# A transformer kernel on one core: a convolution's sums in a PSUM bank, and other lo parts and PSUM banks at six places

## The chip, the cores and the metric

The kernel runs on one core of a Trainium2 chip. The metric is the device time of one execution in microseconds (us). Before the change the median of three runs is 2507.14 us (2504.99 to 2510.89).

The engines' names are those of the profile: PE is TensorE (PEld its weight loads), DVE VectorE, ACT ScalarE, POOL GpSimd, SP the engine that issues most DMAs. Each engine executes its instructions in a fixed order and waits where an operand or a buffer is not ready.

## The reference

Two layers over 512 tokens of width 1024, in fp32. The first block holds an even and an odd layer; each is an attention mixer, a layer norm, an FFN with a squared ReLU and a gated embedding (PLE). The second block is an RWKV7 mixer beside a convolution branch, and another FFN. The convolution branch, which the change touches, is a gated unit and a causal depthwise convolution over 31 tokens:

```
u   = a * sigmoid(b)                    # [tokens, channels], a and b are projections
y_t = bias + sum_{j=0..30} w[:, j] * u_{t-30+j}
```

The gate of the PLE is `x + sigmoid(h @ W_gate + b) * (e @ W_proj)` with a 1024x1024 W_gate.

## The kernel before

**Arithmetic.** Each fp32 product is three fp32r matmuls (mm3, L290 to L292): hi by hi, and the two mixed products of a hi part and a lo part. So each weight needs a hi part (the value rounded to fp32r) and a lo part (the remainder). A weight arrives in parts of 128x1024 values: SP issues the DMA into wraw (L265), ACT writes the hi part whi (L267), and the lo part wlo comes in one of two ways (load_part):

- eng is None: ACT writes the negated hi part into wlo (L270), and POOL's queue issues a DMA (L271) that adds wraw to it on arrival.
- eng is DVE or POOL: that engine subtracts, wraw less whi (L273).

With fast=True the parts of one weight alternate between DVE and POOL, whatever eng is.

**Order.** The tile framework's scheduler writes out one static order for each engine from the program below, its pools' buffer counts and its own costs. A PSUM tag such as psm is a set of banks of 128x512 fp32 values, taken in rotation; a new use waits until the last reader of the old content is done.

**First block.** even_mixer ends with out_proj of ev_w_out, whose second half of columns (256 to 511) is loaded at L782. ffn_and_ple then runs ffn and the gate. The gate's weight comes in two halves of 512 columns (c = 0, 1 at L645 to L647), each in four parts; the first half has fast=True. In ffn, up(0) uses first_two (L419 to L428), which fills two PSUM banks over two halves of the tokens and between them calls the two postponed norms late[0] and late[1]; their transposes (L347) go to psa banks and are copied out by ACT (L351) and DVE (L352). up(1), up(2) and so on take psm banks, which ACT reads with the ReLU (L440). There are three FFNs in the program: two in the first block, one in the second.

**Second mixer.** second_block gives it eight PSUM banks: three psm, one psd, two pst, one psq, one pso (L1721). Eight rounds, one for each 128 channels, weave the RWKV part (projections shifted by shift_add, L1121 and L1122, and wkv_proj, L1449 to L1506) with conv_chunk. In conv_chunk two projections (psd) make the gated unit u (glu, L1401); ACT writes the first tap with the bias into cacc (L1403), and DVE adds the other 30 taps, one instruction each (L1406), 240 in all:

```
    for j in range(1, 31):
        nc.vector.scalar_tensor_tensor(acc, u[:, j:j + 512], cw[:, fc * 31 + j:fc * 31 + j + 1], acc,
                                       op0=ALU.mult, op1=ALU.add)
```

POOL then adds cacc to a running sum (L1343, L1345) and SP stores it.

Of the kernel before, what the change touches and what calls it, by code (L numbers as in the profile page):

```python
# [13 lines left out]
AF = mybir.ActivationFunctionType  # L14
# [274 lines left out]
def mm3(nc, ps, w, x, first, last):  # L289
    nc.tensor.matmul(ps, w[0], x[0], start=first, stop=False)  # L290
    nc.tensor.matmul(ps, w[0], x[1], start=False, stop=False)  # L291
    nc.tensor.matmul(ps, w[1], x[0], start=False, stop=last)  # L292
# [110 lines left out]
def ffn(g, w_up, w_down, X, alpha, hp, tmp, late, norm, fm=None, fill=None):  # L403
# [7 lines left out]
    nc = g.nc  # L411
# [6 lines left out]

    def first_two(W):  # L419

        pss = [g.ps("psm") for _ in range(2)]
        for half, t in enumerate(HALF_TOKENS):
            for e, ps in enumerate(pss):
                for kc in range(8):
                    w = tuple(a[:, e * 128:e * 128 + 128] for a in W[kc])
                    mm3(nc, ps[:, t], w, (X[0][:, kc, t], X[1][:, kc, t]), kc == 0, kc == 7)
                if half == 0:
                    late[e]()  # L428
        return pss
# [162 lines left out]
def ffn_and_ple(g, l, X, late):  # L592

    nc, tc, d = g.nc, g.tc, g.d
    with ExitStack() as s2:
        g.psum(s2, psa=4, psu=2, psm=2)
        pp = g.pool(s2, "ple", 1, side="right")
        up = g.pool(s2, "pleu", 5, side="right")
        pb = g.bcast_row(pp, f"ple_b{l}")
        U = {}  # L600

        def embed(c):

            Wp = g.load_w(d[f"ple_w_proj{l}"][:, c * 512:c * 512 + 512])
            for tb in range(4):
                ps = g.ps("psa")
                for kc in range(2):
                    mm3(nc, ps, tuple(a[:, tb * 128:tb * 128 + 128] for a in P[kc]), Wp[kc], kc == 0, kc == 1)
                U[c, tb] = up.tile([128, 512], F32, name="pu", tag="pu")
                nc.scalar.activation(U[c, tb], ps, AF.Copy, scale=0.5)  # L610

        with ExitStack() as s3:
            hp = g.pool(s3, "hp", 3)
            tmp = g.pool(s3, "ftmp", 1)
            br = g.pool(s3, "brow", 1)
            norm, fm = norm_fm(g, br, l, "ln2", X, "psm", "psm")
            P = []

            def fill():
                P.extend(g.load_w(d["pT"][l]))  # L620
                embed(0)

            late = ffn(g, d[f"w_up{l}"], d[f"w_down{l}"], X, ALPHA, hp, tmp, late, norm, fm, fill)
        tmp = g.pool(s2, "ptmp", 3, side="right")
        if l == 1:
            hn = g.pool(s2, "mhn", 2, side="right")
            gb = g.bcast_row(pp, "norm_mix", "brow2")

        def after(tb):
            if l == 0:  # L630
                to_fm(g, g.x[tb], X, tb)
            else:
                nc.scalar.dma_start(g.xd[tb * 128:tb * 128 + 128, :], g.x[tb])
                ht = hn.tile([128, D], F32, name="hn", tag="hn")
                rms_norm_tm(g, g.x[tb], ht, gb, g.v1[:, V1["eps6"][0]:V1["eps6"][1]])
                to_fm(g, ht, X, tb)

        if l == 0:
            zero = tmp.tile([128, 512], F32, name="zero", tag="pt")
            nc.gpsimd.memset(zero, 0.0)  # L640
            md = g.md.rearrange("k b x -> (k b x)").rearrange("(p x) -> p x", p=128)
            for j in range(0, 1040, 512):
                n = min(512, 1040 - j)
                nc.sync.dma_start(md[:, j:j + n], zero[:, 0:n])
        for c in range(2):  # L645
            cs = slice(c * 512, c * 512 + 512)
            Wg = g.load_w(d[f"ple_w_gate{l}"][:, cs], fast=c == 0, eng=nc.gpsimd)  # L647
            for tb in range(4):
                if c == 0 and 0 < tb < 3:
                    late[tb - 1]()  # L650
                ps = proj_tm(g, Wg, X, tb)
                t = tmp.tile([128, 512], F32, name="pt", tag="pt")
                nc.vector.tensor_tensor(t, ps, pb[:, cs], op=ALU.add)
                nc.scalar.activation(t, t, AF.Tanh, scale=0.5)
                nc.vector.scalar_tensor_tensor(t, t, 1.0, U[c, tb], op0=ALU.add, op1=ALU.mult)
                xs = g.x[tb][:, cs]
                nc.vector.tensor_tensor(xs, xs, t, op=ALU.add)
                if c == 1 and tb > 0:
                    after(tb - 1)
            if c == 0:  # L660
                embed(1)
        after(3)
# [94 lines left out]
def even_mixer(g, outer, late, X, load_x):  # L757
    d, nc = g.d, g.nc
    with ExitStack() as st:
        g.psum(st, psm=2, pst=2, psv=1, pss=3)  # L760
        g.weight_pools(st, 3, 3)
        OT = g.pool(st, "evo", 1).tile([128, 8, 512], F32, name="oT")
        W0 = load_x()
        with ExitStack() as s2:
            a = g.pool(s2, "ev", 1)
            cq, ckv, rq, rkv, rkvb = latents(g, a, X, W0)
            ap = g.pool(s2, "att", 3)
            cs = a.tile([128, 1152], F32, name="cs")
            csk = ap.tile([128, 512], F32, name="tq", tag="tq", bufs=2)
            nc.sync.dma_start(csk, d["ce"][:, OE["cs_k"][0]:OE["cs_k"][1]])  # L770
            nc.sync.dma_start(cs[:, 1024:1152], d["ce"][:, OE["sum4"][0]:OE["sum4"][1]])
            nc.sync.dma_start(cs[:, 0:1024], d["ce"][:, OE["cs_e"][0]:OE["cs_o"][1]])
            win = window_heads(g, a, ap, X, OT)
            lat = latent_heads(g, a, ap, X, OT, cq, ckv, rq, rkv, rkvb, cs, csk)
            units = []
            for p in range(4):
                units += win[2 * p:2 * p + 2] + lat[2 * p:2 * p + 2]
            pipeline(units)
        W = [g.load_w(d["ev_w_out"][:, 0:256])]
        g.alloc_x(outer)  # L780
        g.weight_pools(late, *FFN_W, side="right")
        W.append(g.load_w(d["ev_w_out"][:, 256:512]))  # L782
        load_tokens(g)
        order = [4, 0, 5, 1, 6, 2, 7, 3]
        for j in order:
            split_sb(g, OT[:, j, :], X[0][:, j, :], X[1][:, j, :], nc.vector)
        return out_proj(g, d["ev_w_out"], W, X, ALPHA, "pss", *norm_fm(g, g.pool(st, "evn", 1), 0, "ln1", X, *LATE_TAGS), order)
# [604 lines left out]
def conv_chunk(g, fc, ka, vv, cw, H, cn):  # L1392

    nc, d = g.nc, g.d
    pb = yield from proj_steps(g, d["w_in"][:, 4096 + fc * 128:4224 + fc * 128], H, "psd", fc == 0, fc < 2)
    t = ka.tile([128, 512], F32, name="glt", tag="glt")
    nc.scalar.activation(t, pb, AF.Tanh, scale=0.5)
    pa = yield from proj_steps(g, d["w_in"][:, 3072 + fc * 128:3200 + fc * 128], H, "psd", fc == 0)
    u = ka.tile([128, 542], F32, name="glu", tag="glu")
    nc.vector.memset(u[:, 0:30], 0.0)  # L1400
    nc.vector.scalar_tensor_tensor(u[:, 30:542], t, 1.0, pa, op0=ALU.add, op1=ALU.mult)  # L1401
    acc = ka.tile([128, 512], F32, name="cacc", tag="cacc", bufs=2)
    nc.scalar.activation(acc, u[:, 0:512], AF.Identity, scale=cw[:, fc * 31:fc * 31 + 1],  # L1403
                         bias=vv("conv_b")[:, fc:fc + 1])
    for j in range(1, 31):
        nc.vector.scalar_tensor_tensor(acc, u[:, j:j + 512], cw[:, fc * 31 + j:fc * 31 + j + 1], acc,  # L1406
                                       op0=ALU.mult, op1=ALU.add)
    cn.add(fc, acc)

# [307 lines left out]
def second_block(g, out):  # L1717
    nc, tc, d = g.nc, g.tc, g.d
    with ExitStack() as st:
        with ExitStack() as s2:  # L1720
            g.psum(s2, psm=3, psd=1, pst=2, psq=1, pso=1)  # L1721
            late = second_mixer(g, st)
        g.psum(st, psa=4, psu=2, psm=2)
        hp = g.pool(st, "hp2", 3)
        tmp = g.pool(st, "ftmp2", 1)
        one = g.pool(st, "f2one", 1)
        gf = g.bcast_row(one, "norm_final")

        def norm(tb):
            ht = tmp.tile([128, D], F32, name="hn2", tag="hn2", bufs=3)  # L1730
            rms_norm_tm(g, g.x[tb], ht, gf, g.v1[:, V1["eps6"][0]:V1["eps6"][1]])
            for h in HALVES:
                nc.sync.dma_start(out[tb * 128:tb * 128 + 128, h], ht[:, h])

        ffn(g, d["w_ff1"], d["w_ff2"], g.X, 1.0, hp, tmp, late, norm)
# [21 lines left out]
```

## Time and profile before

| | before |
|---|---|
| median of 3 runs | 2507.14 us (2504.99 to 2510.89) |
| profiled execution | 2508.01 us, its span 2506.2 us |
| mean granted clock of PE | 0.983 |
| PE busy | 2366.2 us (94%) |
| DVE busy | 1517.9 us (61%) |
| ACT busy | 1279.2 us (51%) |
| POOL busy | 1042.2 us (42%) |

The profile is of one execution. Busy times are sums over the span, without the instructions that only wait or issue DMAs. The view of PE's waits lists how long PE stood idle and whose work ended it, as `engine bank line <- engine buffer line: us in total, times, longest`. A granted clock of 1 is TensorE's full speed.

### The profile page before, as it was taken

What the parts mean: (1) busy time and instruction counts of PE and PEld (TensorE: products, weight loads), DVE (VectorE), ACT (ScalarE), POOL (GpSimd) and SP (SyncE); (2) the same over time, 40 slices, a digit from 0 to 9 for tenths busy, and PEclk for the clock granted to TensorE, in tenths of its full rate; (3) what the DMA queues carried; (4) which work ended last, traced back from release to release, by engine and by line L of the source; (5) the groups of instructions that cost most, each with busy time, mean ns of one, the idle gap of its engine ahead of it and who ended that gap; (6) DMA issues with size and microseconds to landing.
All of it is one profiled execution on the core that took longest, in us unless ns stands there. A gap on an engine that the chain in (4) does not pass through costs nothing.

```text
span 2506.2 us, 36411 instructions
## 1 busy us (share of the span) xinstructions
PE 2366.2 (94%) x14140; PEld 1898.9 (76%) x14140; DVE 1517.9 (61%) x2786; ACT 1279.2 (51%) x1999; POOL 1042.2 (42%) x567
## 2 busy tenths in 40 slices
PE   8998999998999999999989998999998999999998
PEld 6778777786777787877768876777765669888776
DVE  3775564667433656564685598777775633555656
ACT  5773444443555645444444454555556644544443
POOL 1113667661110025767631242223344114377772
PEclk9999999999999999999999999999999999999999
DMA  7456232335454343233362476665666458332322
GB/s 207 93 148 173 68 118 84 109 122 147 129 126 108 80 118 111 83 110 93 100 161 74 107 168 137 149 134 127 140 160 147 140 160 254 82 109 84 118 78 74
DMA packets 301485, 309.05 MB, mean 123 GB/s; under 512 B 61184, under 2 KB 234880, under 8 KB 301184
## 3 DMA queue, kind: packets, MB, share of 16 engines
q1 hardware_dynamic: 280432, 239.60, 31.6%
q0 software_dynamic: 20304, 65.02, 14.2%
q8 instruction: 111, 1.82, 0.3%
q10 hardware_dynamic: 576, 2.10, 0.2%
q14 instruction: 62, 0.51, 0.1%
HBM read 221.47 MB, written 20.19 MB: 96 GB/s over the span
## 4 chain that ended last, share of the span: by engine, by line
PE 48%; POOL 14%; DVE 13%; issue 12%; ACT 7%; DMA 6%; POOLq 0%; SPq 0%; DVEq 0%; ACTq 0%
PE psm L290 6%; PE psm L291 6%; PE psm L292 6%; POOL wlo L389 5%; DVE cacc L1406 3%; PE psa L290 3%; PE psa L291 3%; PE psa L292 3%; POOL wlo L273 2%; DMA wlo<-wraw 2%; PE pss L292 2%; PE pss L291 2%; PE pss L290 2%; PE psd L290 2%; PE pst L1415 1%
## 5 line engine op out<-in xcount | busy, mean ns | idle before, releaser
L290 PE MATMUL psm<-xT,whi 128*128 128x512 f32 (+1 forms) x1288 | 503.0, 391 | 24.8 <-ACT hf L440 11.8
L291 PE MATMUL psm<-xT,whi 128*128 128x512 f32 (+1 forms) x1288 | 497.6, 386 | 2.0 <-DVE xT L352 2.0
L292 PE MATMUL psm<-xT,wlo 128*128 128x512 f32 (+1 forms) x1288 | 495.7, 385 | 2.9 <-DMA wlo<-wraw 2.8
L267 ACT ACTIVATE whi<-wraw 128x1024 fp32r<-128x1024 f32 (+3 forms) x287 | 285.5, 1005 | 303.7 <-PE psa L292 102.4
L271 POOL DMA_DIRECT2D wlo<-wraw x141 | 122.8, 873 | 740.0 <-ACT wlo L270 495.1
L273 POOL TENSOR_TENSOR wlo<-wraw,whi 128x1024 fp32r<-128x1024 f32 x124 | 321.2, 2627 | 83.3 <-ACT whi L267 79.6
L389 POOL TENSOR_TENSOR wlo<-wraw,whi 128x1024 fp32r<-128x1024 f32 x84 | 213.2, 2538 | 239.6 <-ACT whi L388 239.6
L290 PEld LDWEIGHTS psm<-xT,whi 128*128 128x128 f32 x1288 | 244.8, 190 | 77.3 <-ACT hf L440 13.1
L292 PEld LDWEIGHTS psm<-xT,wlo 128*128 128x128 f32 x1288 | 244.9, 190 | 50.6 <-DMA wlo<-wraw 4.6
L291 PEld LDWEIGHTS psm<-xT,whi 128*128 128x128 f32 x1288 | 245.3, 190 | 47.6 <-DVE xT L352 3.4
L290 PE MATMUL psa<-whi,hh 128*128 128x512 f32 x600 | 239.0, 399 | 14.9 <-DVE x L460 14.9
L291 PE MATMUL psa<-wlo,hh 128*128 128x512 f32 x600 | 236.7, 395 | 0.0
L292 PE MATMUL psa<-whi,hl 128*128 128x512 f32 x600 | 236.5, 395 | 0.0
L388 ACT ACTIVATE whi<-wraw 128x1024 fp32r<-128x1024 f32 x147 | 151.9, 1053 | 123.6 <-PE psa L292 61.8
L1406 DVE SCALAR_TENSOR_TENSOR cacc<-glu,cw,cacc 128x512 f32<-128x512 f32 x240 | 200.4, 835 | 5.5 <-ACT cacc L1403 1.0
L388 ACT ACTIVATE hh<-hf 128x768 fp32r<-128x768 f32 (+1 forms) x96 | 87.7, 914 | 145.7 <-DVE hf L451 144.0
L389 DVE TENSOR_TENSOR hl<-hf,hh 128x768 fp32r<-128x768 f32 (+1 forms) x96 | 124.3, 1295 | 59.8 <-ACT hh L388 59.8
L290 PEld LDWEIGHTS psa<-whi,hh 128*128 128x128 f32 x600 | 112.9, 188 | 49.1 <-DVE x L460 22.6
L389 DVE TENSOR_TENSOR wlo<-wraw,whi 128x1024 fp32r<-128x1024 f32 x63 | 86.0, 1389 | 93.3 <-ACT whi L388 79.2
L270 ACT ACTIVATE wlo<-whi 128x1024 fp32r<-128x1024 f32 (+3 forms) x141 | 133.8, 952 | 2.3 <-PE psm L292 0.8
L292 PEld LDWEIGHTS psa<-whi,hl 128*128 128x128 f32 x600 | 112.9, 188 | 27.2 <-DVE hl L389 0.7
L291 PEld LDWEIGHTS psa<-wlo,hh 128*128 128x128 f32 x600 | 112.9, 188 | 25.7
(456 smaller groups left out, 5094.4 us busy)
## 6 DMA issues: line engine op xcount, KB each, us to landing
wlo<-wraw POOLq DMA_DIRECT2D x117, 512.0 KB, 5.2
wraw<-in_w_up SPq DMA_DIRECT2D x64, 512.0 KB, 4.5
wraw<-in_w_down SPq DMA_DIRECT2D x64, 512.0 KB, 3.5
wraw<-in_w_ff SPq DMA_DIRECT2D x64, 512.0 KB, 3.7
wraw<-in_w_in SPq DMA_DIRECT2D x56, 512.0 KB, 4.7
wraw<-in_od_w_in SPq DMA_DIRECT2D x24, 512.0 KB, 4.2
wraw<-in_ple_w_gate SPq DMA_DIRECT2D x16, 512.0 KB, 5.7
brow<-in_rows SPq DMA_DIRECT2D x13, 512.0 KB, 6.0
```

What stands on the lines that cost most here:

```text
L267: nc.scalar.activation(hi[:, :m], raw[:, :m], AF.Copy)
L270: nc.scalar.activation(lo[:, :m], hi[:, :m].bitcast(F32), AF.Copy, scale=-1.0)
L271: nc.gpsimd.dma_start(lo[:, :m].bitcast(F32), raw[:, :m], accum_op=ALU.add)
L273: eng.tensor_tensor(lo[:, :m], raw[:, :m], hi[:, :m].bitcast(F32), op=ALU.subtract)
L290: nc.tensor.matmul(ps, w[0], x[0], start=first, stop=False)
L291: nc.tensor.matmul(ps, w[0], x[1], start=False, stop=False)
L292: nc.tensor.matmul(ps, w[1], x[0], start=False, stop=last)
L388: g.nc.scalar.activation(hi, src, AF.Copy)
L389: (eng or g.nc.gpsimd).tensor_tensor(lo, src, hi.bitcast(F32), op=ALU.subtract)
L1406: nc.vector.scalar_tensor_tensor(acc, u[:, j:j + 512], cw[:, fc * 31 + j:fc * 31 + j + 1], acc, op0=ALU.mult, op1=ALU.add)
L1415: nc.tensor.matmul(ps[o], lhs[o], rhs[o], start=start, stop=stop)
```

## The change

Five edits. (1) first_two takes its two banks from psa and no longer from psm; it serves three FFNs. (2) The first half of the gate's columns is loaded with eng None, so that its four parts become an ACT copy and an accumulating DMA each; it happens twice. (3) The second half of ev_w_out is subtracted on POOL; once. These are the six stops. (4) In conv_chunk the running sum lies in a PSUM bank, psc; ACT writes the start there, 29 DVE instructions of a round read and write it, and the 30th writes the result to cacc in SBUF. (5) For that bank the second mixer's psm goes from three banks to two.

```diff
     def first_two(W):
-        pss = [g.ps("psm") for _ in range(2)]
+        pss = [g.ps("psa") for _ in range(2)]
...
-            Wg = g.load_w(d[f"ple_w_gate{l}"][:, cs], fast=c == 0, eng=nc.gpsimd)
+            Wg = g.load_w(d[f"ple_w_gate{l}"][:, cs], eng=nc.gpsimd if c else None)
...
-        W.append(g.load_w(d["ev_w_out"][:, 256:512]))
+        W.append(g.load_w(d["ev_w_out"][:, 256:512], eng=nc.gpsimd))
...
+    part = g.ps("psc")
+    nc.scalar.activation(part, u[:, 0:512], AF.Identity, scale=cw[:, fc * 31:fc * 31 + 1],
+                         bias=vv("conv_b")[:, fc:fc + 1])
     acc = ka.tile([128, 512], F32, name="cacc", tag="cacc", bufs=2)
-    nc.scalar.activation(acc, u[:, 0:512], AF.Identity, scale=cw[:, fc * 31:fc * 31 + 1],
-                         bias=vv("conv_b")[:, fc:fc + 1])
     for j in range(1, 31):
-        nc.vector.scalar_tensor_tensor(acc, u[:, j:j + 512], cw[:, fc * 31 + j:fc * 31 + j + 1], acc,
+        nc.vector.scalar_tensor_tensor(acc if j == 30 else part, u[:, j:j + 512], cw[:, fc * 31 + j:fc * 31 + j + 1], part,
                                        op0=ALU.mult, op1=ALU.add)
...
-            g.psum(s2, psm=3, psd=1, pst=2, psq=1, pso=1)
+            g.psum(s2, psm=2, psd=1, psc=1, pst=2, psq=1, pso=1)
```

One line is added ahead of L1404, so lines after conv_chunk carry a number higher by one in the changed kernel.

On POOL, around the end of even_mixer, the two DMAs of ev_w_out's second half give way to two subtractions ahead of the four that stood there:

```order
 L640 MEMSET zero 128x512
-L271 DMA wlo<-wraw 128x1024 x2
-L273 TENSOR_TENSOR wlo<-wraw,whi 128x1024 x4
+L273 TENSOR_TENSOR wlo<-wraw,whi 128x1024 x6
 L271 DMA wlo<-wraw 128x1024 x4
 L273 TENSOR_TENSOR wlo<-wraw,whi 128x1024 x2
```

The four that follow belong to the first weights of the FFN and move back by two subtractions. On POOL, around the first gate, the gate's two subtractions become DMAs, as do the two parts that DVE had:

```order
 L273 TENSOR_TENSOR wlo<-wraw,whi 128x1024 x6
-L271 DMA wlo<-wraw 128x1024 x3
-L273 TENSOR_TENSOR wlo<-wraw,whi 128x1024 x2
-L271 DMA wlo<-wraw 128x1024 x3
+L271 DMA wlo<-wraw 128x1024 x9
+L273 TENSOR_TENSOR wlo<-wraw,whi 128x1024
+L271 DMA wlo<-wraw 128x1024
 L273 TENSOR_TENSOR wlo<-wraw,whi 128x1024 x3
```

Nothing but DMA issues stands there between the embedding's weights and the gate's. On PE, in the second round of the second mixer (tw and ta are small products of wkv_proj, xT the tokens, ar and bk factors of the state), the order before is:

```order
L1415 MATMUL pst<-ar,bk 64x128 x8
L1449 MATMUL psm<-tw,whi 128x512
L1450 MATMUL psm<-tw,wlo 128x512
L290 MATMUL psm<-xT_61,whi 128x512
L291 MATMUL psm<-xT_62,whi 128x512
L1415 MATMUL pst<-ar,bk 64x128
L1473 MATMUL psm<-ta,whi 128x512
L1474 MATMUL psm<-ta,wlo 128x512
L1484 MATMUL psm<-cb,tmpa 128x2 x4
```

and that of the change:

```order
L1416 MATMUL pst<-ar,bk 64x128 x8
L1450 MATMUL psm<-tw,whi 128x512
L1451 MATMUL psm<-tw,wlo 128x512
L1416 MATMUL pst<-ar,bk 64x128 x5
L290 MATMUL psm<-xT_61,whi 128x512
L291 MATMUL psm<-xT_62,whi 128x512
L1474 MATMUL psm<-ta,whi 128x512
L1475 MATMUL psm<-ta,wlo 128x512
L1416 MATMUL pst<-ar,bk 64x128 x3
```

Four more of the small products on pst now stand ahead of the projection's matmuls and none between these and ta's; the four L1484 come later.

## Rows read from the trace of the kernel before

**Rows 1.** The page, busy time, share of the span and instructions of each engine.
```profile
PE 2366.2 (94%) x14140; PEld 1898.9 (76%) x14140; DVE 1517.9 (61%) x2786; ACT 1279.2 (51%) x1999; POOL 1042.2 (42%) x567
```
**Rows 2.** Waits of PE over the span: us in total, times, longest.
```profile
PE psa L291 <- DVE wlo L273: 12.0, 2, 6.2
PE psm L290 <- ACT hf L440: 11.8, 3, 4.7
...
PE pss L291 <- DMA wlo<-wraw: 7.1, 1, 7.1
...
PE psd L290 <- DVE glu L1401: 4.8, 2, 4.4
...
PE psm L1473 <- DVE v L1122: 4.3, 1, 4.3
...
PE psm L290 <- ACT xT L351: 2.0, 5, 0.7
```
**Rows 3.** Timeline at ev_w_out's second half: start, duration, instruction, [idle before <-releaser].
```profile
181.55 1.04 ACT L267 ACTIVATE whi<-wraw 128x1024 fp32r<-128x1024 f32 x1
...
184.67 1.06 ACT L270 ACTIVATE wlo<-whi 128x1024 fp32r<-128x1024 f32 x1
...
186.25 0.86 POOL L271 DMA_DIRECT2D wlo<-wraw  x1 [1.41 <-DMA wraw<-in_ev_w_out]
...
186.82 7.25 POOL L273 TENSOR_TENSOR wlo<-wraw,whi 128x1024 fp32r<-128x1024 f32 x3
...
193.98 0.58 PE L291 MATMUL pss<-wlo,xT 128*128 128x256 f32 x1 [7.14 <-DMA wlo<-wraw]
```
**Rows 4.** Windows behind five stops: stretch, PE, PEld, DVE, ACT, POOL, PEclk, DMA, GB/s.
```profile
194.00:198.10 4.10, 4.10 (x19) 4.10 (x20) 0.00 (x0) 1.06 (x1) 1.10 (x2) 0.50 1.04 286
...
601.30:604.30 3.00, 3.00 (x7) 2.42 (x8) 2.29 (x3) 2.66 (x3) 0.86 (x1) 0.50 1.07 247
...
1314.00:1317.70 3.70, 3.70 (x9) 2.93 (x10) 3.70 (x13) 0.00 (x0) 0.00 (x0) 0.50 1.06 265
1477.90:1485.00 7.10, 7.10 (x31) 5.98 (x32) 5.85 (x15) 2.75 (x6) 2.72 (x3) 0.52 0.69 175
1526.50:1532.80 6.30, 6.27 (x15) 4.92 (x16) 6.00 (x9) 4.25 (x5) 1.72 (x2) 0.50 1.04 222
```
**Rows 5.** Timeline at the first gate.
```profile
584.91 1.06 ACT L267 ACTIVATE whi<-wraw 128x1024 fp32r<-128x1024 f32 x1
...
592.04 0.86 POOL L271 DMA_DIRECT2D wlo<-wraw  x1 [26.83 <-ACT wlo L270]
...
592.60 4.97 POOL L273 TENSOR_TENSOR wlo<-wraw,whi 128x1024 fp32r<-128x1024 f32 x2
...
593.84 4.95 DVE L374 SCALAR_TENSOR_TENSOR x<-x,bmv,brow 128x512 f32<-128x512 f32 x2
...
600.04 2.35 DVE L273 TENSOR_TENSOR wlo<-wraw,whi 128x1024 fp32r<-128x1024 f32 x2
```
**Rows 6.** Line L271 between 560 and 612 us: from issue to landing.
```profile
DMA to landing us min/median/max: 4.5/5.2/9.0
```
**Rows 7.** Timeline at the second gate.
```profile
1305.20 5.00 POOL L273 TENSOR_TENSOR wlo<-wraw,whi 128x1024 fp32r<-128x1024 f32 x2
```
**Rows 8.** Timeline of a postponed norm in the first FFN.
```profile
240.34 1.38 PE L347 MATMUL psa<-ca,x 128*128 128x128 f32 x8 [0.32 <-DVE x L375]
240.87 2.47 DVE L352 TENSOR_TENSOR xT<-psa,xT 128x512 fp32r<-128x512 f32 x4
```
**Rows 9.** DVE 1415 to 1517 us (busy, mean ns), then ns min/median/max of L1406 and L1122.
```profile
L1406 DVE SCALAR_TENSOR_TENSOR cacc<-glu,cw,cacc 128x512 f32<-128x512 f32 x90 | 77.0, 855 | 2.6 <-ACT cacc L1403 1.0
...
L1406 DVE SCALAR_TENSOR_TENSOR cacc<-glu,cw,cacc x90: 702/752/2309, 1415.9 to 1515.7; 128x512 f32<-128x512 f32 x90
...
L1122 DVE SCALAR_TENSOR_TENSOR v<-psm,v,v x8: 735/744/750, 1411.9 to 1887.1; 128x511 f32<-128x511 f32 x8
```

## The prediction, made before the result was known

> **What bounds the kernel now.** I read the page first: TensorE (PE) is busy for 94% of the span [rows 1]. Work taken from another engine is thus worth nothing by itself; time can only come from the few places where PE stands still, or runs at a lower clock. The second view, the waits of PE, names those places [rows 2]. The change touches five of its lines: psa L291 waiting for a lo part that DVE subtracts (12.0 us, twice: the two gates), psm L290 waiting for ACT's L440 (11.8 us, three times: once per FFN), pss L291 waiting for an accumulating DMA (7.1 us: the second half of ev_w_out), and psd L290 with psm L1473 waiting for DVE in the convolution's rounds (4.4 us the longest, and 4.3 us). [...]
>
> The sum is made against the profiled execution, 2508.01 us; the median of the runs is 2507.14, 0.87 below it. About 0.2%, 5 us, is what a measurement of this kernel can tell from no change.
>
> **ev_w_out, second half.** Before, each of its two parts goes through ACT's hi copy, ACT's negated copy and an issue on POOL. ACT holds the order hi, lo, hi, lo: the second lo copy begins at 184.67, POOL issues its DMA at 186.25, and PE resumes at 193.98, 7.14 us late, when it has landed [rows 3]. After, both parts are subtracted on POOL, first in its queue. Two ACT instructions (1.06 us each) and two DMAs go. The two hi copies of 1.04 follow each other from 181.55 [rows 3], so the second ends at 183.7. POOL's three later subtractions took 7.25 together [rows 3], 2.42 each: the first would end at 185.0, the second at 187.4. PE stopped at 186.84 and would resume at about 187.4: 7.14 less 0.56 = 6.6 saved. The stretch behind the stop, 4.10 us at 0.50 [rows 4], gives back 2.05 if it goes whole. The three POOL subtractions that follow move from 186.82-194.07 to about 187.4-194.7 and still precede the matmuls that use them, which begin only after PE's resumption and the first parts' products. **-8.6**, between 0 (a part of the next weights becomes the wait) and -9.2 (7.14 + 2.05).
>
> **The first gate.** Before, its four parts alternate DVE, POOL, DVE, POOL. POOL stands 26.83 us before the accumulating DMA at 592.04 (it waits for an ACT copy of another weight), and both of its gate subtractions are queued behind that; they run 592.60-597.57 [rows 5]. Beside them DVE's two L374 over 128x512 take 4.95 [rows 5], 2.5 each where L1122, the same operation over 511 columns, takes 0.75 [rows 9]; behind these on DVE stand its own two gate subtractions, 2.35 at 600.04, and PE resumes 6.2 late [rows 2], at 601.3 [rows 4]. After, all four parts are copied and negated by ACT and finished by DMA. Four ACT copies of 1.06 are added, and ACT's 1.06 for a hi copy at 584.91 [rows 5] is the last of the gate's four; in the new order each lo copy stands right behind its hi copy, so the last DMA is issued by about 588.5 (584.9 + 2 x 1.06 + POOL's 0.86, and 0.6 for one eviction between). DMAs issued from that line in this stretch landed in 4.5 to 9.0, median 5.2 [rows 6]: 593.7, at worst 597.5. PE wants the first part at 595.1 (601.3 less 6.2), and the last part, which holds the seventh and eighth of eight chunks of three matmuls, 18 matmuls later. The wait should go: -6.2, and half of the 3.00 us at 0.50 [rows 4] -1.5. **-7.7**, between 0 and -7.7.
>
> **The second gate** is the same picture: POOL's two subtractions take 5.00 at 1305.20 [rows 7], PE stops for 5.8 (12.0 less 6.2, [rows 2]) until 1314.0 and then runs 3.70 at 0.50 [rows 4]: **-7.6**, between 0 and -7.6. The pair of subtractions that DVE no longer does at each gate (2.35) counts in these waits and nowhere else.
>
> **First products of the FFNs in psa.** The 11.8 us [rows 2] do not belong to first_two. They are up(2)'s first product waiting until ACT has read up(1)'s, and up(1) still uses psm in the change, while ACT's order around hf and hh is untouched. Gain 0. Against it, two of the four psa banks are now held, so the second postponed norm's eight transposes at 240.34 [rows 8] need a bank that DVE's L352 (four in 2.47, 0.62 each) has emptied: between 0 and two passes, 1.2. I take one pass, 0.6, three times: **+1.8**.
>
> **The convolution's sum in PSUM.** Nothing is removed: 240 DVE instructions stay, 232 of them now write a PSUM bank, all 240 read it. No DVE instruction of the trace before writes PSUM in this shape. The nearest row that reads PSUM and SBUF, L1122, has the same operation over 511 columns: 735 to 750 ns [rows 9]. The median of L1406 is 752, but the first three chains (90 instructions) have a mean of 855 and a maximum of 2309 [rows 9]: some were stretched, as the gate's L374 was while POOL subtracted beside it [rows 5]. The price lies between 735 (L1122) and 855 (nothing gained); I take 744, L1122's median, since it is the same operation with one input in PSUM. Then the three chains shrink by 90 x 0.111 = 10.0 us on DVE. Those of the other five are under PE's cover; only in the first three does PE wait for DVE [rows 2]. The relief up to the first stop, most of two chains, exceeds its 4.3, so this stop goes with half of its 7.10 us at 0.52 (3.4, [rows 4]): -7.7. The rest of the 10.0 shortens the second stop (4.4) by 10.0 - 7.7 = 2.3, less some of it that lies before the first wait of DVE itself; I take 1.8. **-9.5**, between 0 and -15.3 (both stops and half of 7.10 and of 6.30).
>
> **psm from three banks to two.** That is the price of the new bank: a product in psm now waits for the reader of the product two places before it, and no longer three. L1473's 4.3 us is a wait for such a reader, L1122, and in the new order the product ahead of it meets the same reader with five small matmuls moved up. Bounds: 0, and one such stall with its clock (7.7) in each of eight rounds, 62. I take a short eviction wait, 2.0 / 5 = 0.4 [rows 2], in each round: **+3.2**.
>
> **Sum:** -8.6 - 7.7 - 7.6 + 1.8 - 9.5 + 3.2 = -28.4, so 2508.01 - 28.4 = 2479.6; less the 0.87 of the median, **2479**.
>
> **Rivals.**
> *The banks decide (slower).* If psm's two banks give a stall like L1473's, 4.3 + 3.4 = 7.7, in some rounds: one to three rounds give 2487 to 2502, four 2510, five 2518. The point is 28.4 / 7.7 = 3.7 rounds. For it: L1122 and ACT's readers stand in static orders between conv instructions, and several psm products of a round are only two matmuls long. Against: with three banks only one of eight rounds stalled there [rows 2]. Chance 0.17: 0.09 for one to three, 0.02 for four, 0.06 for five or more.
>
> *PSUM is no cheaper than the stretched SBUF form.* If the 90 instructions keep their 855, by a dearer PSUM operand or because the stretching stays, the -9.5 goes: 2489. For it: no row writes PSUM. Against: L1122's 735 to 750 with a PSUM input, never stretched in its eight [rows 9]. Chance 0.14.
> [...]
>
> *The gates' DMAs land late.* If ACT's copies come only where the stretch's own next lo copy stood before (the DMA at 592.04 [rows 5]), landings of 5.2 to 9.0 end at 597 to 601 and PE waits as long as before: the two gate terms vanish, 2479 + 15.3 = 2494. For it: the landing's 9.0 [rows 6], and a queue of nine DMAs on POOL. Against: ACT's new order. Chance 0.15.
> [...]
>
> *The next wait takes the place.* All three removed stops are followed by work that needs other late weights (the FFN's, the gate's second half on POOL). If each gives its time to the next, -23.9 goes: 2503, no change. Against: right behind the three stops PE is busy for 4.10 of 4.10, 3.00 of 3.00 and 3.70 of 3.70 us [rows 4]. Chance 0.06.
>
> **How the numbers follow.** The forecast has the remaining 0.48, with its own range 2470 to 2487. Faster by over 0.2%: 0.48 + 0.14 + 0.15 + 0.09 + 0.01 of the last = 0.87; within 0.2%: 0.02 + 0.05 = 0.07; slower 0.06. The range: at the low end no bank cost (3.2), no first_two cost (1.8) and both conv stops gone (5.8 more) give 2468, put at 2467; the high end, 2501, takes in the gates, the PSUM price and up to three bank stalls. Left out: 0.14 above, 0.04 below.
>
> **What would show it.** Right: the lines psa L291 <- DVE wlo and pss L291 <- DMA wlo vanish from PE's waits, the windows behind them show a clock near 1; the conv line has a mean near 745 with no instruction over 800; the ACT hf L440 line stays near 11.8; psm waits for L1122 or ACT readers in the rounds grow by 3. Wrong: a mean of 800 or more on the conv line, psa L292 or L291 waiting for DMA wlo at the gates, or psm waits of over 15 us in the rounds, which would turn the result.

## The result and the profile after

The changed kernel takes 2482.26 us (median of 4 runs, 2480.82 to 2483.55) against 2506.4 for the kernel before (median of 4). The ratio is 0.9899, 95% interval 0.9883 to 0.9915: 25 us less, 21 to 29 (the two medians differ by 24). The forecast was 2479 in a range of 2467 to 2501. The profiled execution took 2481.95 us, its span 2479.8, 26 below that of before. Gains and losses of the experiments below, in us, are worked out from their ratios, with the kernel before at 2506 us; where a stretch of a trace is compared, the numbers are of one profiled execution each.

The page shows that PE did the same work, with a little less standing still (the line answers to [rows 1]):

```profile
PE 2364.9 (95%) x14140; PEld 1898.6 (77%) x14140; DVE 1481.9 (60%) x2782; ACT 1283.0 (52%) x2005; POOL 1030.6 (42%) x571
```

PE's waits, answering to [rows 2] (us in total, times, longest):

```profile
PE psa L290 <- DVE x L460: 15.5, 14, 1.7
PE psm L290 <- ACT hf L440: 12.3, 3, 4.7
...
PE psm L292 <- DMA wlo<-wraw: 5.4, 3, 2.4
...
PE psd L292 <- DMA wlo<-wraw: 2.8, 2, 1.6
PE psa L291 <- DMA wlo<-wraw: 2.3, 3, 1.0
...
PE psa L347 <- DVE xT L352: 1.4, 1, 1.4
...
PE psa L291 <- POOL wlo L273: 1.0, 2, 0.7
```

The lines psa L291 <- DVE wlo (12.0), pss L291 <- DMA wlo (7.1) and psm L1473 <- DVE v (4.3) are gone, and psd L290 <- DVE glu has fallen from 4.8 to 0.6. What took the places of the long stops is short: 2.3 and 1.0 at the gates, and 0.62 at ev_w_out, where PE now resumes at 187.45 behind POOL's subtraction (timeline of PE, then of POOL):

```profile
187.45 0.39 PE L291 MATMUL pss<-wlo,xT 128*128 128x256 f32 x1 [0.62 <-POOL wlo L273]
...
182.66 14.16 POOL L273 TENSOR_TENSOR wlo<-wraw,whi 128x1024 fp32r<-128x1024 f32 x6 [24.90 <-PE pss L290]
```

One kind of wait grew, and it lies elsewhere: PE at L292 for a lo part that a DMA brings. The kernel before had

```profile
PE psm L292 <- DMA wlo<-wraw: 2.8, 3, 1.8
...
PE psd L292 <- DMA wlo<-wraw: 1.0, 2, 0.8
```

and of the 8.2 us now, 6.6 are in the convolution's rounds, against 2.1 of the 3.8 before.

The clock behind the removed stops is whole, where [rows 4] had 0.50. The windows are at ev_w_out, the first and the second gate (PE, PEld, DVE, ACT, POOL, PEclk, DMA share, GB/s):

```profile
186.80:194.00 7.20, 6.58 (x55) 6.55 (x55) 2.07 (x5) 2.42 (x3) 7.20 (x4) 1.00 1.03 333
...
590.00:618.00 28.00, 24.67 (x117) 19.87 (x115) 9.66 (x16) 14.00 (x19) 5.65 (x4) 1.00 0.52 119
1288.00:1353.00 65.00, 62.00 (x310) 51.26 (x308) 38.96 (x71) 36.23 (x53) 14.11 (x8) 1.00 0.43 116
```

The convolution's instructions (ns min/median/max, answering to [rows 9]) cost what they cost before when undisturbed, and none is stretched any more. All 240 together take 179.7 us on DVE, 173.8 for those that write psc and 5.9 for the eight that write cacc. The changed kernel first, then the kernel before, all 240 and those from the fourth gated unit on:

```profile
L1407 DVE SCALAR_TENSOR_TENSOR psc<-glu,cw,psc x232: 665/754/758, 1392.7 to 1799.3; 128x512 f32<-128x512 f32 x116
L1407 DVE SCALAR_TENSOR_TENSOR cacc<-glu,cw,psc x8: 727/742/748, 1419.1 to 1800.2; 128x512 f32<-128x512 f32 x8
```

```profile
L1406 DVE SCALAR_TENSOR_TENSOR cacc<-glu,cw,cacc 128x512 f32<-128x512 f32 x240 | 200.4, 835 | 5.5 <-ACT cacc L1403 1.0
...
L1406 DVE SCALAR_TENSOR_TENSOR cacc<-glu,cw,cacc 128x512 f32<-128x512 f32 x150 | 123.5, 823 | 2.9
```

The two traces also show what ran beside those that were stretched. Before, 43 of the 240 overlap in time with a TENSOR_TENSOR of POOL, its arithmetic; these average 1237 ns, and all 25 that took over 800 ns are among them. The other 197 average 747 ns and never pass 755. In the changed kernel 49 overlap with POOL in the same way, and their longest is 758. The longest of before, 2309 ns, is the first of the two in the second row here (timeline of POOL, then of DVE):

```profile
1421.53 2.88 POOL L389 TENSOR_TENSOR wlo<-ka,whi 128x1024 fp32r<-128x1024 f32 x1 [3.57 <-ACT whi L388]
...
1422.66 3.10 DVE L1406 SCALAR_TENSOR_TENSOR cacc<-glu,cw,cacc 128x512 f32<-128x512 f32 x2
```

The second mixer in two stretches is the one surprise. The first stretch runs from the first gated unit (L1401) to the mean of the convolution (L1350), the second from there to where ACT begins to wait for the last FFN's first eviction (L440), some 4 us before it takes place. The columns are those above. Of before, and then of the changed kernel:

```profile
1414.20:1842.90 428.70, 406.82 (x3369) 308.10 (x3367) 349.84 (x788) 239.80 (x399) 135.88 (x120) 0.98 0.63 142
1842.90:2155.60 312.70, 291.09 (x2615) 230.23 (x2615) 154.62 (x410) 159.09 (x276) 102.41 (x78) 0.97 0.62 168
```

```profile
1391.00:1803.70 412.70, 401.73 (x3377) 304.83 (x3375) 325.22 (x788) 238.88 (x399) 127.18 (x120) 0.99 0.66 145
1803.70:2126.90 323.20, 298.72 (x2609) 235.85 (x2609) 154.50 (x410) 159.32 (x276) 100.25 (x78) 0.94 0.61 164
```

The rounds are 16.0 us shorter and the part behind them 10.5 longer, with as many matmuls. Of the 10.5, 7.6 are PE busy longer (the granted clock is 0.94 for 0.97, and 3% of 323 us is 9.7) and 2.9 are PE standing still. The pattern is that of all the kernels here: behind the rounds the granted clock is 0.97 or 0.98 in the six with the sum in SBUF, and 0.94 to 0.96 in the eight with the sum in PSUM.

### The profile page after: what moved, and what is told of

Its sections match the earlier page's. It is cut to its first block, busy times and chain, and to the rows that moved or that the text cites. A ratio compares the mean times of both kernels' runs of the same rounds, so it can differ in the third digit from the quotient of the medians.

```text
span 2479.8 us, 36415 instructions
## 1 busy us (share of the span) xinstructions
PE 2364.9 (95%) x14140; PEld 1898.6 (77%) x14140; DVE 1481.9 (60%) x2782; ACT 1283.0 (52%) x2005; POOL 1030.6 (42%) x571
## 4 chain that ended last, share of the span: by engine, by line
PE 55%; POOL 13%; issue 11%; DVE 9%; DMA 6%; ACT 6%; SPq 0%; POOLq 0%; DVEq 0%; ACTq 0%
PE psm L290 7%; PE psm L291 7%; PE psm L292 7%; POOL wlo L389 4%; PE psa L290 4%; PE psa L291 4%; PE psa L292 4%; POOL wlo L273 3%; DMA wlo<-wraw 2%; PE pst L1416 2%; PE psd L290 2%; PE pss L292 2%; PE pss L291 2%; PE pss L290 2%; PE psd L292 2%
## 5 line engine op out<-in xcount | busy, mean ns | idle before, releaser
L290 PE MATMUL psm<-xT,whi 128*128 128x512 f32 (+1 forms) x1192 | 476.2, 400 | 23.3 <-ACT hf L440 12.3
L292 PE MATMUL psm<-xT,wlo 128*128 128x512 f32 (+1 forms) x1192 | 469.7, 394 | 5.4 <-DMA wlo<-wraw 5.4
L291 PE MATMUL psm<-xT,whi 128*128 128x512 f32 (+1 forms) x1192 | 471.0, 395 | 0.5 <-DVE xT L352 0.5
L271 POOL DMA_DIRECT2D wlo<-wraw x147 | 127.3, 872 | 729.0 <-ACT wlo L270 497.4
L273 POOL TENSOR_TENSOR wlo<-wraw,whi 128x1024 fp32r<-128x1024 f32 x122 | 315.5, 2620 | 102.0 <-ACT whi L267 73.4
L389 POOL TENSOR_TENSOR wlo<-wraw,whi 128x1024 fp32r<-128x1024 f32 x84 | 212.9, 2534 | 241.9 <-ACT whi L388 241.9
L290 PEld LDWEIGHTS psm<-xT,whi 128*128 128x128 f32 x1192 | 226.7, 190 | 74.7 <-ACT hf L440 13.6
L292 PEld LDWEIGHTS psm<-xT,wlo 128*128 128x128 f32 x1192 | 226.6, 190 | 53.1 <-DMA wlo<-wraw 6.5
L291 PEld LDWEIGHTS psm<-xT,whi 128*128 128x128 f32 x1192 | 227.4, 191 | 44.6 <-DVE xT L352 0.9
L290 PE MATMUL psa<-whi,hh 128*128 128x512 f32 x600 | 239.0, 398 | 15.6 <-DVE x L460 15.5
L291 PE MATMUL psa<-wlo,hh 128*128 128x512 f32 x600 | 236.6, 395 | 0.0
L292 PE MATMUL psa<-whi,hl 128*128 128x512 f32 x600 | 236.4, 395 | 0.0
L1407 DVE SCALAR_TENSOR_TENSOR psc<-glu,cw,psc 128x512 f32<-128x512 f32 x232 | 173.8, 749 | 5.9 <-ACT psc L1403 2.2
L290 PEld LDWEIGHTS psa<-whi,hh 128*128 128x128 f32 x600 | 112.8, 188 | 49.7 <-DVE x L460 23.1
L270 ACT ACTIVATE wlo<-whi 128x1024 fp32r<-128x1024 f32 (+3 forms) x147 | 140.1, 956 | 2.3 <-PE psm L292 0.7
L292 PEld LDWEIGHTS psa<-whi,hl 128*128 128x128 f32 x600 | 112.8, 188 | 27.2 <-DVE hl L389 0.7
L291 PEld LDWEIGHTS psa<-wlo,hh 128*128 128x128 f32 x600 | 112.8, 188 | 25.8
```

The costliest lines, as they stand in the source:

```text
L270: nc.scalar.activation(lo[:, :m], hi[:, :m].bitcast(F32), AF.Copy, scale=-1.0)
L271: nc.gpsimd.dma_start(lo[:, :m].bitcast(F32), raw[:, :m], accum_op=ALU.add)
L273: eng.tensor_tensor(lo[:, :m], raw[:, :m], hi[:, :m].bitcast(F32), op=ALU.subtract)
L389: (eng or g.nc.gpsimd).tensor_tensor(lo, src, hi.bitcast(F32), op=ALU.subtract)
L1407: nc.vector.scalar_tensor_tensor(acc if j == 30 else part, u[:, j:j + 512], cw[:, fc * 31 + j:fc * 31 + j + 1], part, op0=ALU.mult, op1=AL ...
```

## The experiments

The first four take the change apart: the convolution with its bank, the bank alone, the six stops alone, and the change without first_two.

**The convolution alone** has edits 4 and 5 and none of the others.

```diff
+    part = g.ps("psc")
...
+        nc.vector.scalar_tensor_tensor(acc if j == 30 else part, ..., part,
-            g.psum(s2, psm=3, psd=1, pst=2, psq=1, pso=1)
+            g.psum(s2, psm=2, psd=1, psc=1, pst=2, psq=1, pso=1)
```

> Only the convolution's sum in PSUM with psm at two banks; the six stops are as before. By the prediction's terms (-9.5 + 3.2) the time is some 6 us under the kernel before: 2498 to 2503, with the eight rounds up to the mean of the convolution shorter by 15 to 20 us and the part of the mixer behind them longer by about 10, as in the changed kernel's trace. Rival: the loss behind the rounds comes with the six stops and not with the convolution; then the rounds' gain stays whole and the time is 2488 to 2492. Second rival: without the stops the rounds gain nothing; 2505 or more.

2505.52 us, ratio 0.9992 (0.9981 to 1.0002): 2 us less, and the interval takes in no change; 2498 to 2503 were expected. The two stretches of the mixer:

```profile
1415.60:1825.60 410.00, 399.67 (x3375) 303.37 (x3373) 323.55 (x788) 238.58 (x399) 127.72 (x120) 1.00 0.66 146
1825.60:2150.70 325.10, 298.42 (x2609) 235.62 (x2609) 154.13 (x410) 159.20 (x276) 101.01 (x78) 0.94 0.60 163
```

The rounds gain 18.7 and the part behind them loses 12.4, at the clock of 0.94 again. So the loss comes with the convolution and not with the six stops.

The mixer as a whole is 6.3 us shorter in this execution (735.1 for 741.4), more than the 2 us of the ratio. Over more traces the 6 holds: with the sum in SBUF and three banks of psm the mixer takes 738.8 to 742.2 in five kernels (before, and four of the runs below), with the change's mixer 731.4 to 735.9 in four (the change, this run, the one without first_two and the one with two buffers for hf); the means, 740.6 and 734.5, are 6.1 apart. The ratio of this run does not reach that, so the size of the convolution's gain is known only as some 2 to 6 us.

Where the rounds gain is seen when they are parted at the fourth gated unit, which leaves three rounds ahead of it and five behind. Before, and then the convolution alone:

```profile
1414.20:1525.80 111.60, 101.93 (x485) 80.54 (x483) 104.36 (x175) 58.44 (x89) 40.12 (x34) 0.97 0.64 142
1525.80:1842.90 317.10, 304.90 (x2884) 227.55 (x2884) 245.48 (x613) 181.36 (x310) 95.76 (x87) 0.99 0.63 141
```

```profile
1415.60:1517.80 102.20, 98.73 (x485) 77.72 (x483) 93.63 (x174) 56.04 (x86) 36.32 (x33) 1.00 0.69 154
1517.80:1825.60 307.80, 300.94 (x2897) 225.64 (x2892) 229.92 (x615) 182.55 (x313) 91.40 (x87) 0.99 0.65 144
```

The first three rounds gain 9.4 us and the other five 9.3.

**The bank alone** leaves the sum in SBUF and gives psm two banks.

```diff
-            g.psum(s2, psm=3, psd=1, pst=2, psq=1, pso=1)
+            g.psum(s2, psm=2, psd=1, pst=2, psq=1, pso=1)
```

> psm at two banks in the second mixer and the sum still in SBUF; the eighth bank is left unused. If the gain of the rounds is DVE's time, this kernel has none of it and pays the banks: 2506 to 2514 (prediction's +3.2, with room for one stall). Rival: the gain is the other order that two banks bring; then 2494 to 2502 with the conv instructions still stretched to a mean of 835.

2512.68 us, ratio 1.0022 (1.0011 to 1.0032): 5.5 us more. Its stretches, and its convolution (busy us and mean ns):

```profile
1416.20:1850.30 434.10, 406.86 (x3369) 304.32 (x3367) 350.81 (x789) 239.66 (x399) 134.54 (x120) 0.98 0.62 140
1850.30:2160.50 310.20, 291.00 (x2617) 228.69 (x2617) 156.26 (x409) 159.77 (x276) 102.06 (x78) 0.98 0.62 169
```

```profile
L1406 DVE SCALAR_TENSOR_TENSOR cacc<-glu,cw,cacc 128x512 f32<-128x512 f32 x240 | 199.6, 832 | 5.7 <-ACT cacc L1403 1.3
```

The rounds are 5.4 longer and the part behind them is 2.5 shorter. So two banks are not what speeds the rounds, nor what slows the part behind them. Against this kernel the sum in PSUM is worth 434.1 - 410.0 = 24.1 us in the rounds, while DVE's own saving is 199.6 - 179.7 = 19.9. The two kernels differ in more than DVE's time, though: with the sum in PSUM the scheduler also writes another order for PE. No run parts the one from the other.

**The six stops alone** are edits 1 to 3.

```diff
-        pss = [g.ps("psm") for _ in range(2)]
+        pss = [g.ps("psa") for _ in range(2)]
...
-            Wg = g.load_w(d[f"ple_w_gate{l}"][:, cs], fast=c == 0, eng=nc.gpsimd)
+            Wg = g.load_w(d[f"ple_w_gate{l}"][:, cs], eng=nc.gpsimd if c else None)
...
-        W.append(g.load_w(d["ev_w_out"][:, 256:512]))
+        W.append(g.load_w(d["ev_w_out"][:, 256:512], eng=nc.gpsimd))
```

> The six stops alone, the second mixer as before. The prediction's terms give -8.6 - 7.7 - 7.6 + 1.8 = -22.1: 2482 to 2487, and the three PE stops of 5.8 to 7.1 us gone. Rival: the changed kernel's stops gained only because the mixer was moved too; then 2490 or more. With the first experiment: if the parts add up, the two differences together give the changed kernel's 2482.

2488.66 us, ratio 0.9928 (0.9912 to 0.9944): 18 us less, 14 to 22, where the terms had 22.1. With the convolution's 2 that is 20; the whole change shows 25, with an interval of 4 either way. The parts add up within what the runs can tell. The long stops at the gates and at ev_w_out are gone in this kernel, and the two of the convolution stand (5.5 and 4.4 us).

**Without first_two**: the change, with the two banks from psm as before.

```diff
-        pss = [g.ps("psa") for _ in range(2)]
+        pss = [g.ps("psm") for _ in range(2)]
```

> The whole change but for first_two, which keeps psm. The prediction has psa for first_two at a loss of 1.8: 2478 to 2481 against 2482.3 for the whole change, with the waits of PE for L440 the same (11.8 to 12.3 us). Rival: psa spares a wait for banks; then 2484 or more.

2485.55 us, ratio 0.9914 (0.9898 to 0.9931), 3.8 us above the whole change, where 2 below were expected: the time is the rival's. But the intervals overlap, so neither is shown. The waits for L440 are 11.9, so that half of the expectation held.

The next three are the stops one by one. **The gates alone:**

```diff
-            Wg = g.load_w(d[f"ple_w_gate{l}"][:, cs], fast=c == 0, eng=nc.gpsimd)
+            Wg = g.load_w(d[f"ple_w_gate{l}"][:, cs], eng=nc.gpsimd if c else None)
```

> Only the gate's first half by ACT copies and accumulating DMAs, in both layers. The prediction's terms are -7.7 and -7.6: 2489 to 2493 with the kernel before at 2506.5, PE's waits for DVE wlo L273 (12.0 us) gone and no wait for DMA wlo over 2 us at the gates. Rival (late landings): 2498 or more, with PE waiting there for DMA wlo.

2494.98 us, ratio 0.9948 (0.9935 to 0.9961): 13 us less, 10 to 16. The time read is above the expected range, for the most part because before read 2508.2 beside it; by the ratio the terms' 15.3 lies inside the interval. The wait that remains at the gates is short:

```profile
PE psa L291 <- DMA wlo<-wraw: 2.3, 3, 0.9
```

**ev_w_out alone:**

```diff
-        W.append(g.load_w(d["ev_w_out"][:, 256:512]))
+        W.append(g.load_w(d["ev_w_out"][:, 256:512], eng=nc.gpsimd))
```

> Only the second half of ev_w_out subtracted on POOL. The prediction's term is -8.6, the changed kernel's trace showed -7.0 by the start of the FFN: 2497 to 2501, PE's 7.1 us for DMA wlo gone. Rival: the FFN's weights become the next wait and give it back: 2504 or more.

2500.14 us, ratio 0.9967 (0.9955 to 0.9979): 8.3 us less. The rival, that the FFN's weights become the next wait, is out.

**first_two alone:**

```diff
-        pss = [g.ps("psm") for _ in range(2)]
+        pss = [g.ps("psa") for _ in range(2)]
```

> Only first_two's banks from psa. The prediction's term is +1.8: 2507 to 2510, with waits of the postponed norms' transposes for L352 of some 0.6 us in each FFN and the 11.8 us for L440 unchanged. Rival: psa takes a bank wait away; 2501 to 2505.

2511.03 us, ratio 1.0009 (1.0000 to 1.0017): 2.2 us more, as the term of 1.8 had it. But the mechanism is not seen well: psa L347 <- DVE L352 is 1.5 us here where the kernel before has 1.1, not 0.6 in each FFN. Alone the edit costs some 2 us; inside the change it seemed to gain 4. Nothing larger than the scatter of either is shown.

**The tail of the mixer.** Here a theory was to be tried: with the rounds shorter, the serial steps of the state behind them have too little PE work beside them. One projection of a branch gate was moved from round 7 to round 8, and then two were moved.

```diff
-GATES = (0, 1, 1, 2, 2, 2, 2, 2, 4)
+GATES = (0, 1, 1, 2, 2, 2, 2, 1, 5)
```

> The whole change, and one projection of a branch gate (24 matmuls, some 5.5 us of PE) moved from the second mixer's round 7 to round 8, by the table that spreads them. Theory: the rounds' gain (17 us by the mean of the convolution) is given back behind them because the serial steps of the state have too little PE work beside them there, so PE stops for 1 to 3 us and falls to the lower clock; with one projection more these stops shrink: 2474 to 2479 against 2482.3. Rival: the loss is not a lack of cover (the clock, or another order); the projection only changes place: 2481 to 2486.

2479.65 us, ratio 0.9879 (0.9859 to 0.9898). With two moved, one each from rounds 6 and 7, (0, 1, 1, 2, 2, 2, 1, 1, 6):

> The whole change, and two projections of branch gates moved to round 8, one each from rounds 6 and 7. If the tail lacks cover, the second projection gives less than the first or as much (the first gave 2482.3 to 2479.7): 2473 to 2480. Rival: the first gave nothing but scatter, or the rounds miss the work now: 2481 to 2488.

2484.94 us, ratio 0.9900 (0.9886 to 0.9913). The stretches with one, and with two moved:

```profile
1398.50:1810.70 412.20, 401.34 (x3375) 304.65 (x3373) 324.58 (x788) 237.28 (x399) 128.05 (x120) 0.99 0.65 145
1810.70:2129.30 318.60, 292.66 (x2609) 234.09 (x2609) 157.00 (x410) 160.80 (x277) 103.45 (x77) 0.96 0.61 167
```

```profile
1393.10:1812.20 419.10, 404.34 (x3441) 307.20 (x3440) 328.31 (x798) 238.14 (x404) 129.49 (x121) 0.98 0.64 143
1812.20:2128.80 316.60, 290.73 (x2546) 232.28 (x2544) 150.57 (x401) 160.74 (x271) 99.28 (x76) 0.96 0.62 167
```

Two moved give nothing over the change: the sum of the stretches is 735.7 against 735.9. One moved gives 730.8 in this execution and 5 us by the ratios (0.9879 against 0.9899), but the two intervals overlap, and the change's own mixer took 731.4, at a clock of 0.96 behind the rounds, in the run without first_two. So neither shows a gain.

Nor was the theory put to the test, for neither edit brought more PE work behind the rounds. Rounds 7 and 8 both lie behind the mean of the convolution, so with one moved the second stretch has the same 2609 matmuls as in the changed kernel, in another order. With two moved, one projection crosses the mean, but the mean itself stands later in PE's order, and the second stretch has 2546 matmuls, 63 fewer. Why PE runs longer at the lower clock behind the rounds, once the sum is in PSUM, stays open; that DVE is sooner done there and that PE's order is another are both possible.

**Two buffers for hf.** The prediction said that PE's waits for L440 belong to ACT, held by hf and hh. The whole change, with one line more:

```diff
-        F = tmp.tile([128, 8, 256], F32, name="hf", tag="hf")
+        F = tmp.tile([128, 8, 256], F32, name="hf", tag="hf", bufs=2)
```

> The whole change, and two buffers for hf in the FFNs. The prediction says that PE's wait for L440 (12.3 us in three) comes from ACT, held by hf and hh, and not from PSUM banks. ACT's order stays, and only L440's own wait for DVE's reader of hf (1.35 us in the first FFN) can go: 1.4 in each FFN and half as much of clock behind it, 2476 to 2480 against 2482.3, with the L440 line at 7 to 9 us. Rival: the wait is one for the other operands; 2481 to 2484 and 12 us.

2456.78 us, ratio 0.9789 (0.9776 to 0.9802), some 28 us below the change by the ratios, far more than either reading. The L440 line of PE's waits is 8.6, within what was expected. The rest lies in the body of the FFNs. ACT's row for L440 (busy, mean ns, idle before) and the first FFN's window from the third unit on, in the changed kernel:

```profile
L440 ACT ACTIVATE hf<-psm 128x512 f32<-128x512 f32 x90 | 52.9, 588 | 128.5 <-PE psm L292 101.2 <-DVE hl L389 27.3
```

```profile
255.10:555.60 300.50, 293.69 (x1265) 238.41 (x1266) 177.10 (x188) 144.11 (x174) 206.62 (x81) 0.99 0.33 104
```

and with two buffers, where PE's waits come with them:

```profile
L440 ACT ACTIVATE hf<-psm 128x512 f32<-128x512 f32 x90 | 52.5, 583 | 95.3 <-PE psm L292 95.3
```

```profile
257.30:547.40 290.10, 289.89 (x1258) 236.89 (x1257) 175.25 (x187) 141.19 (x171) 205.94 (x81) 1.00 0.34 107
```

```profile
PE psm L290 <- ACT hf L440: 8.6, 3, 3.8
...
PE psa L290 <- DVE x L460: 0.4, 2, 0.2
```

L440 waited 27.3 us in all for DVE's last reader of the only hf buffer. Behind it, PE's waits psa L290 <- DVE x L460 (15.5 us in 14) go as well: they name DVE's L460, but it was the hold on hf that made DVE and ACT late. No other order explains it: PE's and POOL's are the same in the two programs, and in the first FFN's window DVE's and ACT's are too. Of the 10.4 us that this window is shorter, 6.6 are PE standing still (0.2 us, not 6.8) and 3.8 are PE busy for less time, at a clock of 1.00 and not 0.99. The other two FFNs are shorter by 11.0 and 10.0 in the same way. That makes 31.4 us; the spans differ by 25.2 (2479.8 and 2454.6), so some 6 are lost outside these windows.

**The parts that gained, together**: one gate projection in round 8, two buffers for hf, and first_two in psm or in psa.

```diff
-GATES = (0, 1, 1, 2, 2, 2, 2, 2, 4)
+GATES = (0, 1, 1, 2, 2, 2, 2, 1, 5)
...
-        F = tmp.tile([128, 8, 256], F32, name="hf", tag="hf")
+        F = tmp.tile([128, 8, 256], F32, name="hf", tag="hf", bufs=2)
...
-        pss = [g.ps("psa") for _ in range(2)]
+        pss = [g.ps("psm") for _ in range(2)]
```

> One gate projection in round 8, two buffers for hf, and first_two back in psm, with the rest of the change. If the three add up (-2.6, some -4, and -2.2 by the run of first_two alone): 2472 to 2476. Rival: first_two's psa gains inside the whole change (the run without it gave 2485.6): 2477 to 2483, slower than the next kernel.

2452.41 us, ratio 0.9769 (0.9755 to 0.9782). With psa, that is without the last two lines of the diff:

> The same with first_two in psa: 2474 to 2479 if the parts add up, 2 us above the kernel with psm; under it by 2 to 4 if psa gains inside the whole change.

2455.62 us, ratio 0.9779 (0.9765 to 0.9792). Both lie far below their expectations, for the most part because hf was expected at some -4; between them nothing can be told. The first has the lowest ratio of all the kernels here, 2.3% under the kernel before, though its interval meets that of the two buffers alone.

## Why the prediction was right, point by point

| term | predicted, us | measured, us | from |
|---|---|---|---|
| ev_w_out on POOL | -8.6 | -8.3 (-11.3 to -5.3) | 0.9967 |
| gates by ACT and DMA | -15.3 | -13.0 (-16.3 to -9.8) | 0.9948 |
| first_two in psa | +1.8 | +2.2 (0 to +4.3) | 1.0009 |
| psm at two banks | +3.2 | +5.5 (+2.8 to +8.0) | 1.0022 |
| convolution with its bank | -6.3 | -2.0 (-4.8 to +0.5) | 0.9992 |
| the change | -28.4 | -25.3 (-29.3 to -21.3) | 0.9899 |

The forecast of the whole came out, and so did the two terms that make up most of it. The convolution's steps did not, and there the sum was right by luck.

**ev_w_out** held in its steps: PE was to resume at 187.4 and resumed at 187.45, and the window behind it went from 0.50 to a clock of 1.00. The prediction took half of each stretch at 0.50 or 0.52 as lost, an estimate from that clock, and the windows come near it: 19 matmuls in 4.10 us at 0.50 are 216 ns each, 55 in 6.58 at 1.00 are 120, so 1.8 us of the 4.10 was lost, where the term had 2.05.

**The gates** held. The DMAs landed somewhat later than [rows 6]: between 560 and 600 us the median is 6.6 (4.5 to 8.9), at the second gate, between 1265 and 1305 us, 7.4 (up to 10.2). The price was three waits of 1.0 us at most. The rival of late landings did not decide; the trace shows later landings without a reason for them.

**first_two.** That its edit would leave the L440 waits as they are was right: 11.8 before, 12.3 after. Its own price, alone, is of the size named, but the step behind it (a wait of 0.6 in each FFN) is not seen: PE's wait for L352 in psa grew by 0.4 in all.

**The convolution** is where the steps failed. Its term with the bank, -9.5 + 3.2 = -6.3, agrees with the traces, in which the mixer is 741.4 - 735.9 = 5.5 us shorter; by the time of the kernel with the convolution alone it is -2.0, and that interval leaves -6.3 out. The price of an instruction was right in kind: 754 ns, beside L1122's 744 and L1406's own 752, and no longer stretched. So the rival with a dearer PSUM operand is out for these operands.

That the stretching would go was taken from L1122's row alone. The trace bears it out without a reason for it: beside POOL's arithmetic the instructions with two inputs in SBUF reached 2309 ns, those with one at most 758.

One step failed, one was mis-sized and one was missing. The step that failed is "those of the other five are under PE's cover; only in the first three does PE wait for DVE". The three chains that [rows 9] shows were not special: the other five have a mean of 823 ns. Nor are they covered. In the last five rounds of the kernel before PE waits for DVE too, though in short pieces (PE's waits from 1525.8 to 1842.9):

```profile
PE psd L290 <- DVE glu L1401: 4.8, 2, 4.4
PE pst L1415 <- DVE nn L1622: 4.2, 3, 1.4
PE psq L1660 <- DVE s L1654: 1.4, 3, 0.7
...
PE psm L290 <- DVE rs L1489: 0.8, 1, 0.8
PE psq L1415 <- DVE st L1674: 0.7, 3, 0.3
```

The 4.4 is the second stop, which the prediction counted; some 9 us of waits for DVE are left beside it, and with the convolution alone 1.3 of them remain. The first three rounds gained 9.4 us, near the 9.5 of the prediction; the five gained 9.3, 5.3 of it in PE standing still, where it had nothing. Mis-sized was the banks' price: 0.4 in each round, 3.2 in all, against 5.4 in the rounds of the kernel with the bank alone and 5.5 by its ratio, though 3.2 is just inside that interval. And no step looked behind the rounds, where the kernel with the convolution alone loses 12.4 us, 7.3 of them by PE being busy longer at the lower clock. In that kernel's trace the three make the forecast's number: -24.1 by the sum in PSUM in the rounds, +5.4 by the banks, +12.4 behind, -6.3 in all. That errors of opposite sign met there is luck.

**The rivals.** The banks as what decides (slower) did not come: 5.5 us is less than one full stall of 7.7. The next wait in place of the old ones did not come at ev_w_out and the gates. In the convolution's rounds it did in part, as the waits for lo parts by DMA (6.6 us for 2.1), and more is lost behind them, where the prediction had not looked.

## What to carry to other kernels

Price a stop by its own length and by the clock behind it (0.50 for 3.0 to 4.1 us at ev_w_out and the gates), and then find the instruction whose order makes the operand late; at the stops with one such cause the sum held within 3 us. For work that runs through many rounds, add up the short waits as well as the long stops, and look also at the stretch that follows: here it lost more than half of what the rounds gained (10.5 us of 16.0). And read the idle time of an evicting engine by releaser: the single hf buffer held L440 for 27.3 us in all, and a second one was worth some 28, where PE's list had 12.3 under its name.

## What the runs showed that was not expected

- The DVE instruction with one input in PSUM and its output there took 754 ns over 128x512 (median), like the SBUF form's 752. Beside POOL's arithmetic it was never over 758, where the SBUF form averaged 1237 and reached 2309.
- With the sum in PSUM the mixer's rounds are 16 to 19 us shorter in the change and in the convolution alone, and the part behind them is 10 to 12 us longer with as many matmuls, at a granted clock of 0.94 and not 0.97. The cause is not shown.
- One more buffer for hf was worth some 28 us, as much as the whole change, by a hold that PE's waits listed under DVE's L460.
